# One ScalarE copy empties the value products' bank, and branch B's halves are added by accumulating loads

## The chip, the cores and the metric

The kernel runs on one core of a Trainium2 chip. The metric is device time in microseconds of one execution, as the median of several runs. Lower is better.

The engines are named as in the profile: PE is TensorE's matrix multiplication and PEld its loading of weights (the stationary operand), DVE is VectorE, ACT is ScalarE, POOL is GpSimd, and SP is SyncE, which only issues DMAs. A small q behind a name means the engine's queue of instructions (its sequencer).

## The reference, cut to what matters

One layer of a streaming encoder is computed for a prompt of 1024 frames and a sample of 64 frames. Two branches run beside each other, both fed by one input projection, and their outputs are gated, summed and projected again. Branch A is a gated linear recurrence. Branch B is causal softmax attention with 16 heads of 64 channels and a forget gate in the logits:

```python
def fox_attend(q, k, v, cq, ck, qpos, kpos):
    s = jnp.einsum('qhd,khd->hqk', q, k).astype(jnp.float32) * (HEAD_DIM ** -0.5)
    s = s + cq.astype(jnp.float32).T[:, :, None] - ck.astype(jnp.float32).T[:, None, :]
    s = jnp.where((kpos[None, :] <= qpos[:, None])[None], s, -jnp.inf)
    p = jax.nn.softmax(s, axis=-1)
    return jnp.einsum('hqk,khd->qhd', p.astype(v.dtype), v)
...
    yb = yb.reshape(B, L, W_B) * jax.nn.silu(gb)
    u = jnp.einsum('bsnw,nwd->bsnd', jnp.stack([ya, yb], axis=2), w_branch)
```

The change touches the last line of `fox_attend` (the value products) and the way from there to `yb * silu(gb)`.

## The kernel before, in words

All matrix products are made in float32 precision from operands that are split into a high and a low half: a product takes the passes high*high, high*low and low*high. High halves are written by ScalarE (a copy that rounds, line 90), low halves by a subtraction on VectorE (line 93).

**Attention.** Work is cut into 64 units `(head, q2)`: one head with 256 queries, in the order q2 = 0, 3, 1, 2 for each head. A unit has three kinds of steps on TensorE. *Scores* (lines 1212 and 1213) put logits into a PSUM bank; VectorE adds the mask and takes the least of the negated logits (line 1184), ScalarE takes the exponential (line 1191), and GpSimd inverts the row sum by a power (line 1193) and scales (line 1194). *Turns* transpose up to four blocks of 128x128 probabilities (line 1244); ScalarE writes the high half `th` of the transposed block and VectorE the low half `tl`. *Values* (`values`, lines 1265 and 1267) multiply these with the values.

In the value products the stationary operand `vv` holds the high half of the head's values in columns 0 to 63 and the low half in columns 64 to 127. So a product of 128 output rows by 256 queries holds two partial sums: rows 0 to 63 and rows 64 to 127. The output of the head is the sum of the two. Before the change, a unit's product goes into one half (256 columns) of a single PSUM bank, `pv`; `pv_half` hands the two halves out in turn. After the unit's last value step ScalarE copies rows 64 to 127 to the tile `lo`, VectorE adds rows 0 to 63 and `lo` into the tile `y` of 64 rows (line 1293), and GpSimd's queue stores `y` to DRAM, to `d_y` (line 1297). The sample's product (once for two heads, `sample_values`) is emptied by two small ScalarE copies and two small VectorE additions (line 1345).

**The planner.** ScalarE's, VectorE's and GpSimd's order in attention, and TensorE's through the whole kernel, are the order in which the program issues instructions. A loop in the program chooses the next TensorE step with estimated times. `book(engine, at, ns, do)` finds a free place of `ns` nanoseconds on an engine from time `at` on, puts the instruction on the agenda, and returns its end plus 90 ns. A step may go when its inputs are due; a unit's first value step also waits for a free room, whose times stand in `v_free` (two rooms). Where no step is due, TensorE takes a part of a *filler*: an input-projection panel (lines 179 to 181), whose results are stored and used later. The figures such as `A_LO`, `D_Y` and `G_INV` are the planner's estimates in ns and issue nothing by themselves.

**Branch A, then branch B's rows.** After attention come branch A and its eight output panels a0 to a7 (products with `ya`). Their results are multiplied by a gate on VectorE (line 1864) into four buffers `st_a`, and stored by GpSimd's queue (line 1865). Beside them the rows of branch B are prepared, eight tiles of 128 channels by 1088 frames. For each tile, `branch_in` loads `t` from `d_y` (line 1820) and `z` from `d_gb` (line 1821) on SP's queue. VectorE multiplies `t` by `z` (line 1837, or line 1855 for the first two tiles), then by sigmoid(z) (line 1826); ScalarE writes the high half `ybh` and VectorE the low half `ybl`. Tiles 0 and 1 are loaded ahead into rooms of their own; tiles 2 to 7 use two buffers (`yb_in`, `gb_in`) in turn. The first panel of branch B needs all eight tiles within its first 4 us. The weights of each panel are split into `wh` and `wl` on ScalarE and VectorE one panel ahead. In this part the scheduler of the language orders the queues of SP, VectorE, ScalarE and GpSimd by its own estimate of when each instruction is ready; only TensorE's order is that of the program. An accumulating DMA (`accum_op`) adds what it reads to what its destination holds; it is issued by GpSimd. The kernel before has eleven of them, for weights of branch A (line 297).

Of the kernel before, what the change touches and what calls it, by code (L numbers as in the profile page):

```python
# [14 lines left out]
P = 128  # L15
# [23 lines left out]
GC = 364  # L39

HOP_PE, HOP = 250.0, 90.0
D_MAX, D_LO, D_Y, D_YS = (240.0, 1.035), (130.0, 1.1), 420.0, 230.0
A_EXP, A_HI, A_LO, A_ST, A_W = (450.0, 0.85), (150.0, 0.88), 380.0, 470.0, 1060.0
G_NORM, G_INV = (260.0, 0.84), 220.0
G_DMA = 860.0
D_W = 1240.0

# [26 lines left out]
def hybrid_step(tc, a, o):  # L74
# [24 lines left out]
    d_cq = dram.tile([2, NH, DEC], F32, name="d_cq")  # L99
    d_ma = dram.tile([KT, P, T], F32, name="d_ma")  # L100
    d_mb = dram.tile([KT, P, T], F32, name="d_mb")
    d_y = dram.tile([NP, P, T], F32, name="d_y")
    d_gb = dram.tile([KT, P, T], F32, name="d_gb")
    d_ga = dram.tile([KT, P, T], F32, name="d_ga")
    d_x = [dram.tile([P, T], F32, name=f"d_x{k}") for k in range(2)]
# [930 lines left out]
    def book(engine, at, ns, do=None):  # L1036

        busy = booked[engine]
        while busy and busy[0][1] < now[0] - 20000.0:
            busy.pop(0)  # L1040
        i = 0
        while i < len(busy) and busy[i][0] < at + ns:
            at = max(at, busy[i][1])
            i += 1
        busy.insert(i, (at, at + ns))
        if do is not None:
            serial[0] += 1
            heapq.heappush(agenda, (at, serial[0], do))
        return at + ns + HOP
# [201 lines left out]
        return book("D", at, per(D_LO, n), lambda: sub(dve, tl[:, :n], tp[:, :n], f(th[:, :n])))  # L1251

    pvs = {}
    lo_free = [0.0]
    def values(u, g, h, q2):
        vv = heads_v[h]
        if g == 0:
# [27 lines left out]
            part(0, tl, start=False, stop=False)  # L1285
        high_part(0, True)
        spent(460.0)
        lo = p2.tile([HD, 256], F32, name="lo", tag="lo", bufs=1)
        y = p2.tile([HD, 256], F32, name="y", tag="y", bufs=3)

        dst = d_y[h // 2][(h % 2) * HD:(h % 2 + 1) * HD, q2 * 256:(q2 + 1) * 256]
        at = book("A", max(now[0] + HOP_PE, lo_free[0]), A_LO, lambda: copy_act(lo[:, :], pv[HD:, :256]))
        at = book("D", at, D_Y, lambda: dve.tensor_tensor(out=y[:, :], in0=pv[:HD, :256], in1=lo[:, :], op=ALU.add))
        v_free.popleft()
        v_free.append(at)
        lo_free[0] = at
        book("G", at, G_DMA, lambda: pool.dma_start(dst, y[:, :]))


# [30 lines left out]
    def sample_values(p):  # L1330
        t = smp.pop(p)
        pv = pv_half()
        for i in range(2):
            pe.matmul(pv[:, :], t["vs"][:, i, 0, :], t["pt"][:, i, :, :].rearrange("p s n -> p (s n)"),
                      start=(i == 0), stop=False)
            pe.matmul(pv[:, :P], t["vs"][:, i, 1, :], t["pt"][:, i, 0, :], start=False, stop=(i == 1))
        spent(458.0)
        ys = p2.tile([P, DEC], F32, name="ys", tag="ys", bufs=1)
        ats = []
        for j in range(2):  # L1340
            js, ks = slice(j * HD, (j + 1) * HD), slice(P + j * HD, P + (j + 1) * HD)
            ats.append(book("A", now[0] + HOP_PE, per(A_HI, HD), lambda js=js, ks=ks: copy_act(ys[js, :], pv[js, ks])))
        for j, at in enumerate(ats):
            js = slice(j * HD, (j + 1) * HD)
            at = book("D", at, D_YS, lambda js=js: dve.tensor_tensor(out=ys[js, :], in0=pv[js, js], in1=ys[js, :],
                                                                     op=ALU.add))
        book("D", at, 0.0, lambda: sp.dma_start(d_y[p][:, SEQ:], ys[:, :]))
        v_free.popleft()
        v_free.append(at)

# [19 lines left out]
    due = {}  # L1372
    s_free = deque([0.0, 0.0, 0.0])
    t_free = deque([0.0, 0.0])
    v_free = deque([0.0, 0.0])
    prs = {}
    seen = {"t": 0, "v": 0}
    last_t = {u: ("t", u, q2) for u, (h, q2) in enumerate(units)}
# [438 lines left out]
        return ybpool.tile([P, T], dt, name=name, tag=f"yb{i}{k}")  # L1817

    def branch_in(k, t, z):
        sp.dma_start(t[:, :], d_y[k])  # L1820
        sp.dma_start(z[:, :], d_gb[k])
        return t, z

# [574 lines left out]
```

## Time and profile before

| | |
|---|---|
| median of 3 runs | 1430.43 us (1429.32 to 1431.48) |
| the profiled execution | 1429.49 us, its span 1427.5 us |
| mean granted TensorE clock | 0.998 |
| busy: PE, PEld | 1410.8 us, 1358.0 us |
| busy: DVE, ACT, POOL | 899.4 us, 720.5 us, 436.5 us |
| attention's value products | from 470.9 us to 845 us |
| loads of branch B's rows (line 1820) | issued from 1017.8 us to 1090.8 us |
| first product of branch B's panels | at 1110.8 us |

The span is the time from the first to the last instruction in the profile; the execution's own time is 2.0 us more. Rows of a timeline give the start in us from the span's start, the duration in us, the engine, the line, and `out<-in`; in brackets stands idle time before the instruction, and what ended it. Rows of groups give busy time in us and mean ns of one, then idle time before. A releaser is inferred from semaphore events. Matmuls are pipelined, so the distance between two starts tells more than a matmul's own duration.

### The profile page before, as it was taken

What the parts mean: (1) busy time and instruction counts of PE and PEld (TensorE: products, weight loads), DVE (VectorE), ACT (ScalarE), POOL (GpSimd) and SP (SyncE); (2) the same over time, 40 slices, a digit from 0 to 9 for tenths busy, and PEclk for the clock granted to TensorE, in tenths of its full rate; (3) what the DMA queues carried; (4) which work ended last, traced back from release to release, by engine and by line L of the source; (5) the groups of instructions that cost most, each with busy time, mean ns of one, the idle gap of its engine ahead of it and who ended that gap; (6) DMA issues with size and microseconds to landing.
All of it is one profiled execution on the core that took longest, in us unless ns stands there. A gap on an engine that the chain in (4) does not pass through costs nothing.

```text
span 1427.5 us, 25022 instructions
## 1 busy us (share of the span) xinstructions
PE 1410.8 (99%) x9217; PEld 1358.0 (95%) x9217; DVE 899.4 (63%) x1638; ACT 720.5 (50%) x1339; POOL 436.5 (31%) x652
## 2 busy tenths in 40 slices
PE   9999999999999999999999999999999999999997
PEld 8999999999999999999999999999999999888887
DVE  5564766564432666666666656898767474777654
ACT  5423544442222666666666657777544232565443
POOL 0012322233204777768776841221011000000001
PEclk9999999999999999999999999999999999999999
DMA  6667556765247764556566545564467774224211
GB/s 225 214 133 107 150 155 193 162 180 141 85 122 194 182 130 131 137 110 151 123 150 131 84 101 106 83 101 84 165 211 264 252 237 136 113 74 150 78 48 45
DMA packets 138919, 201.20 MB, mean 141 GB/s; under 512 B 24372, under 2 KB 98844, under 8 KB 137772
## 3 DMA queue, kind: packets, MB, share of 16 engines
q1 hardware_dynamic: 119436, 158.96, 44.2%
q0 software_dynamic: 8160, 23.25, 5.9%
q10 hardware_dynamic: 11200, 17.38, 3.4%
q8 instruction: 73, 1.20, 0.3%
q14 instruction: 50, 0.41, 0.1%
HBM read 131.60 MB, written 66.36 MB: 139 GB/s over the span
## 4 chain that ended last, share of the span: by engine, by line
PE 82%; DVE 6%; DMA 5%; ACT 3%; issue 3%; POOL 1%; SPq 0%; DVEq 0%; ACTq 0%; POOLq 0%
PE quad L844 17%; PE acc L179 11%; PE acc L181 11%; PE acc L180 11%; PE q L2042 5%; PE tp L1244 4%; PE pv L1265 3%; PE s L1213 2%; PE s L1212 2%; PE pv L1267 2%; PE vacc L179 1%; PE vacc L180 1%; PE vacc L181 1%; DMA w_raw<-in_w_in 1%; PE vacc L500 1%
## 5 line engine op out<-in xcount | busy, mean ns | idle before, releaser
L179 PE MATMUL acc<-xh,wh 128*128 128x364 f32 x720 | 237.6, 330 | 0.2 <-ACT st L90 0.2
L181 PE MATMUL acc<-xh,wl 128*128 128x364 f32 x720 | 235.8, 328 | 0.0
L180 PE MATMUL acc<-xl,wh 128*128 128x364 f32 x720 | 235.8, 327 | 0.0
L179 PEld LDWEIGHTS acc<-xh,wh 128*128 128x128 f32 x720 | 135.4, 188 | 1.2 <-ACT st L90 0.5
L180 PEld LDWEIGHTS acc<-xl,wh 128*128 128x128 f32 x720 | 135.3, 188 | 0.8
L181 PEld LDWEIGHTS acc<-xh,wl 128*128 128x128 f32 x720 | 135.1, 188 | 0.0
L90 ACT ACTIVATE wh<-w_raw 128x1024 fp32r<-128x1024 f32 (+1 forms) x66 | 63.4, 962 | 86.4 <-PE quad L844 34.4
L93 DVE TENSOR_TENSOR wl<-w_raw,wh 128x1024 fp32r<-128x1024 f32 (+1 forms) x55 | 62.5, 1138 | 67.6 <-ACT wh L90 47.0
L1193 POOL TENSOR_TENSOR sm<-sm,warm 128x1 f32<-128x1 f32 x136 | 79.2, 582 | 57.0 <-ACT pb L1191 21.8
L93 DVE TENSOR_TENSOR tl<-tp,th 128x512 fp32r<-128x512 f32 x96 | 65.6, 687 | 38.7 <-ACT th L90 37.9
L844 PE MATMUL quad<-xh,wh 128*128 128x272 f32 x416 | 87.4, 291 | 1.8 <-ACT p__3330 L90 1.8
L844 PE MATMUL quad<-xl,wh 128*128 128x272 f32 x416 | 86.1, 288 | 0.0
L844 PE MATMUL quad<-xh,wl 128*128 128x272 f32 x416 | 86.0, 288 | 0.0
L1191 ACT ACTIVATE pb<-pb,nm 128x896 f32<-128x896 f32 (+1 forms) x64 | 63.3, 989 | 24.0 <-DVE nm L1184 21.3
L90 ACT ACTIVATE th<-tp 128x512 fp32r<-128x512 f32 x96 | 56.4, 592 | 31.0 <-PE tp L1244 30.3
L2338 POOL TENSOR_TENSOR junk<-ple,g_ple 128x256 f32<-128x256 f32 x4 | 3.8, 956 | 213.2 <-DVE ple L2295 213.2
L1212 PE MATMUL s<-k,q 128*128 128x128 f32 (+2 forms) x192 | 67.5, 353 | 0.0
L844 PEld LDWEIGHTS quad<-xh,wh 128*128 128x128 f32 x416 | 65.3, 188 | 2.3 <-ACT p__3330 L90 2.0
L1213 PE MATMUL s<-k,q 68*128 68x128 f32 (+2 forms) x192 | 65.3, 344 | 0.5 <-issue 0.5
L844 PEld LDWEIGHTS quad<-xh,wl 128*128 128x128 f32 x416 | 65.5, 188 | 0.0
L844 PEld LDWEIGHTS quad<-xl,wh 128*128 128x128 f32 x416 | 65.4, 188 | 0.0
L1194 POOL TENSOR_SCALAR pb<-pb,sm 128x896 f32<-128x896 f32 (+1 forms) x64 | 61.5, 962 | 6.2
(744 smaller groups left out, 4230.4 us busy)
## 6 DMA issues: line engine op xcount, KB each, us to landing
w_raw<-in_w_in SPq DMA_DIRECT2D x56, 256.0 KB
q<-d_q SPq DMA_DIRECT2D x48, 256.0 KB
k<-d_k SPq DMA_DIRECT2D x48, 256.0 KB
w_raw<-in_w_in SPq DMA_DIRECT2D x64, 128.0 KB
w_raw<-in_w_branch SPq DMA_DIRECT2D x32, 256.0 KB
wl<-w_raw POOLq DMA_DIRECT2D x11, 512.0 KB, 4.5
wraw<-in_w_in SPq DMA_DIRECT2D x20, 256.0 KB
d_k<-oh ACTq DMA_DIRECT2D x16, 272.0 KB
```

Source lines behind the costliest of these rows:

```text
L90: return act.activation(out=out, in_=in_, func=AF.Copy, scale=scale)
L93: return eng.tensor_tensor(out=out, in0=in0, in1=in1, op=ALU.subtract)
L179: pe.matmul(out, ah, bh, start=start, stop=False)
L180: pe.matmul(out, ah, bl, start=False, stop=False)
L181: pe.matmul(out, al, bh, start=False, stop=stop)
L844: pe.matmul(acc[:, c, :CW], l[:, k, :], r[:, k, c * CW:(c + 1) * CW], start=(first and k == 0 and p == 0), stop=(k == 3 and p == 2), skip_ ...
L1191: at = book("A", at, per(A_EXP, n), lambda: act.activation(out=pr[:, :n], in_=pr[:, :n], func=AF.Exp, scale=-1.0, bias=nm, accum_out=sm))
L1193: at = book("G", at, G_INV, lambda: pool.tensor_tensor(out=sm, in0=sm, in1=warm[:, :], op=ALU.pow))
L1194: return book("G", at, per(G_NORM, n), lambda: pool.tensor_scalar(out=pr[:, :n], in0=pr[:, :n], scalar1=sm, scalar2=1.0, op0=ALU.mult, op1 ...
L1212: pe.matmul(s[:, :w], t["q1"][:, q0:q0 + P], t["k1"][:, c], start=True, stop=False)
L1213: pe.matmul(s[:, :w], t["q2"][:HD + 4, q0:q0 + P], t["k2"][:HD + 4, c], start=False, stop=True)
L2042: pe.matmul(acc, l[:, k, :], r[:, k, :], start=(first and k == 0 and i == 0), stop=(k == 3 and i == 2), skip_group_check=not first)
```

## The change

The planner keeps one room for the value products, `v_free = deque([0.0])`, where it kept two; the bank and `pv_half` stay. After a unit's last value step ScalarE copies all 128 rows of the product to `y`, now a tile of 128 rows; VectorE's addition and the tile `lo` go. The store takes both halves: `d_y` has a place for each pair of heads, each head of it, 128 rows and 1024 frames. For the sample one copy of 128x256 replaces the two small ones, the two small additions read the copy in SBUF, and the result goes to a tensor of its own, `d_ys`. The planner's figure for the inversion, `G_INV`, goes from 220 to 570 ns.

In `branch_in`, the one load of `t` becomes three on SP's queue (rows 0 to 63 of the two heads' products, and the sample's columns), and two accumulating loads on GpSimd's queue add rows 64 to 127. `z` is loaded as before.

```diff
@@ -39,9 +39,9 @@
 GC = 364
 
 HOP_PE, HOP = 250.0, 90.0
-D_MAX, D_LO, D_Y, D_YS = (240.0, 1.035), (130.0, 1.1), 420.0, 230.0
-A_EXP, A_HI, A_LO, A_ST, A_W = (450.0, 0.85), (150.0, 0.88), 380.0, 470.0, 1060.0
-G_NORM, G_INV = (260.0, 0.84), 220.0
+D_MAX, D_LO, D_YS = (240.0, 1.035), (130.0, 1.1), 230.0
+A_EXP, A_HI, A_Y, A_ST, A_W = (450.0, 0.85), (150.0, 0.88), 380.0, 470.0, 1060.0
+G_NORM, G_INV = (260.0, 0.84), 570.0
 G_DMA = 860.0
 D_W = 1240.0
 
@@ -99,7 +99,8 @@
     d_cq = dram.tile([2, NH, DEC], F32, name="d_cq")
     d_ma = dram.tile([KT, P, T], F32, name="d_ma")
     d_mb = dram.tile([KT, P, T], F32, name="d_mb")
-    d_y = dram.tile([NP, P, T], F32, name="d_y")
+    d_y = dram.tile([NP, 2, P, SEQ], F32, name="d_y")
+    d_ys = dram.tile([NP, P, DEC], F32, name="d_ys")
     d_gb = dram.tile([KT, P, T], F32, name="d_gb")
     d_ga = dram.tile([KT, P, T], F32, name="d_ga")
     d_x = [dram.tile([P, T], F32, name=f"d_x{k}") for k in range(2)]
@@ -1251,7 +1252,6 @@
         return book("D", at, per(D_LO, n), lambda: sub(dve, tl[:, :n], tp[:, :n], f(th[:, :n])))
 
     pvs = {}
-    lo_free = [0.0]
     def values(u, g, h, q2):
         vv = heads_v[h]
         if g == 0:
@@ -1285,15 +1285,11 @@
             part(0, tl, start=False, stop=False)
         high_part(0, True)
         spent(460.0)
-        lo = p2.tile([HD, 256], F32, name="lo", tag="lo", bufs=1)
-        y = p2.tile([HD, 256], F32, name="y", tag="y", bufs=3)
-
-        dst = d_y[h // 2][(h % 2) * HD:(h % 2 + 1) * HD, q2 * 256:(q2 + 1) * 256]
-        at = book("A", max(now[0] + HOP_PE, lo_free[0]), A_LO, lambda: copy_act(lo[:, :], pv[HD:, :256]))
-        at = book("D", at, D_Y, lambda: dve.tensor_tensor(out=y[:, :], in0=pv[:HD, :256], in1=lo[:, :], op=ALU.add))
+        y = p2.tile([P, 256], F32, name="y", tag="y", bufs=3)
+        dst = d_y[h // 2, h % 2][:, q2 * 256:(q2 + 1) * 256]
+        at = book("A", now[0] + HOP_PE, A_Y, lambda: copy_act(y[:, :], pv[:, :256]))
         v_free.popleft()
         v_free.append(at)
-        lo_free[0] = at
         book("G", at, G_DMA, lambda: pool.dma_start(dst, y[:, :]))
 
 
@@ -1335,18 +1331,16 @@
                       start=(i == 0), stop=False)
             pe.matmul(pv[:, :P], t["vs"][:, i, 1, :], t["pt"][:, i, 0, :], start=False, stop=(i == 1))
         spent(458.0)
+        yv = p2.tile([P, 256], F32, name="y", tag="y", bufs=3)
         ys = p2.tile([P, DEC], F32, name="ys", tag="ys", bufs=1)
-        ats = []
+        at = book("A", now[0] + HOP_PE, A_Y, lambda: copy_act(yv[:, :], pv[:, :256]))
+        v_free.popleft()
+        v_free.append(at)
         for j in range(2):
             js, ks = slice(j * HD, (j + 1) * HD), slice(P + j * HD, P + (j + 1) * HD)
-            ats.append(book("A", now[0] + HOP_PE, per(A_HI, HD), lambda js=js, ks=ks: copy_act(ys[js, :], pv[js, ks])))
-        for j, at in enumerate(ats):
-            js = slice(j * HD, (j + 1) * HD)
-            at = book("D", at, D_YS, lambda js=js: dve.tensor_tensor(out=ys[js, :], in0=pv[js, js], in1=ys[js, :],
-                                                                     op=ALU.add))
-        book("D", at, 0.0, lambda: sp.dma_start(d_y[p][:, SEQ:], ys[:, :]))
-        v_free.popleft()
-        v_free.append(at)
+            at = book("D", at, D_YS, lambda js=js, ks=ks: dve.tensor_tensor(
+                out=ys[js, :], in0=yv[js, js], in1=yv[js, ks], op=ALU.add))
+        book("D", at, 0.0, lambda: sp.dma_start(d_ys[p], ys[:, :]))
 
 
 
@@ -1372,7 +1366,7 @@
     due = {}
     s_free = deque([0.0, 0.0, 0.0])
     t_free = deque([0.0, 0.0])
-    v_free = deque([0.0, 0.0])
+    v_free = deque([0.0])
     prs = {}
     seen = {"t": 0, "v": 0}
     last_t = {u: ("t", u, q2) for u, (h, q2) in enumerate(units)}
@@ -1817,7 +1811,11 @@
         return ybpool.tile([P, T], dt, name=name, tag=f"yb{i}{k}")
 
     def branch_in(k, t, z):
-        sp.dma_start(t[:, :], d_y[k])
+        for j in range(2):
+            sp.dma_start(t[j * HD:(j + 1) * HD, :SEQ], d_y[k, j][:HD, :])
+        sp.dma_start(t[:, SEQ:], d_ys[k])
+        for j in range(2):
+            pool.dma_start(t[j * HD:(j + 1) * HD, :SEQ], d_y[k, j][HD:, :], accum_op=ALU.add)
         sp.dma_start(z[:, :], d_gb[k])
         return t, z
 
```

## The prediction

> **What bounds the kernel now.** I read the page first: shares of the engines, then the chain that ended last.
>
> ```profile
> span 1427.5 us, 25022 instructions
> PE 1410.8 (99%) x9217; PEld 1358.0 (95%) x9217; DVE 899.4 (63%) x1638; ACT 720.5 (50%) x1339; POOL 436.5 (31%) x652
> PE 82%; DVE 6%; DMA 5%; ACT 3%; issue 3%; POOL 1%; SPq 0%; DVEq 0%; ACTq 0%; POOLq 0%
> ```
>
> TensorE is busy 99% of the span, 16.7 us of it idle, and carries 82% of the chain. No engine's relief shows in the end time unless TensorE waits for it. So I looked at the two stretches that the change touches, in the table by stretch: attention, and the end of branch A, where branch B's rows are loaded.
>
> ```profile
> 460.00:850.00 390.00, 388.38 (x2706) 377.93 (x2705) 247.42 (x658) 252.47 (x578) 277.72 (x455) 1.00 0.58 131
> 1060.00:1120.00 60.00, 60.00 (x362) 60.00 (x362) 38.14 (x45) 22.02 (x22) 9.18 (x17) 1.00 0.76 250
> ```
>
> Columns: stretch, length, then busy us and instructions of PE, PEld, DVE, ACT, POOL; clock, DMA share, GB/s. Attention leaves TensorE 1.6 us idle in 390, and the loading stretch none, at full clock. There, DMA is at 0.76 of its time, and POOL has 51 us free. What TensorE and its weight loads wait for in attention is the whole list below (waits, 460 to 860 us: total, times, longest), TensorE's own row first.
>
> ```profile
> PE pv L1265 <- DVE y L1293: 1.2, 4, 0.5
> PEld pv L1265 <- DVE y L1293: 2.1, 4, 0.7
> PEld pv L1267 <- DVE y L1293: 1.4, 4, 0.4
> PEld pv L1267 <- ACT lo L90: 0.2, 1, 0.2
> PEld pv L1265 <- DVE ys L1345: 0.2, 1, 0.2
> ```
>
> Every wait is for the emptying of the value products' bank. That is all this part of the change can remove: 1.2 us if only TensorE's idle counts, 3.9 us if the weight loads' does.
>
> **The emptying, part by part.** The groups by shape (460 to 850 us) price what goes and what comes.
>
> ```profile
> L90 ACT ACTIVATE lo<-pv 64x256 f32<-64x256 f32 x64 | 24.4, 382 | 20.4 <-PE pv L1265 9.4 <-PE pv L1267 7.9 <-PE pv L1336 1.2
> L90 ACT ACTIVATE ys<-pv 64x64 f32<-64x64 f32 x16 | 3.4, 213 | 0.4 <-DVE y L1293 0.3
> L90 ACT ACTIVATE pts<-tps 128x256 fp32r<-128x256 f32 x8 | 3.0, 379 | 0.1
> L1293 DVE TENSOR_TENSOR y<-pv,lo 64x256 f32<-64x256 f32 x64 | 26.4, 412 | 32.9 <-ACT lo L90 11.9 <-PE pv L1265 7.8 <-ACT st L90 3.9
> ```
>
> DVE loses its 64 additions: 26.4 us busy, and up to the 32.9 us that its queue stood still before them. Nothing on TensorE waits for another DVE operation here, so it is worth nothing by itself. ScalarE goes from 64 x 382 + 16 x 213 ns = 27.9 us to 72 copies of 128x256 at 379 ns = 27.3 us: no change. The 16 small sample additions stay on DVE and read the copy instead of PSUM; their DVE work is hidden as before.
>
> Does a single room cost anything against two? A stretch of the timeline answers.
>
> ```profile
> 504.63 0.38 ACT L90 ACTIVATE lo<-pv 64x256 f32<-64x256 f32 x1
> 505.47 0.37 PE L1265 MATMUL pv<-tl,vv 128*128 128x256 f32 x1
> 505.67 0.28 PE L1265 MATMUL pv<-th,vv 128*128 128x256 f32 x1
> 505.91 0.28 PE L1265 MATMUL pv<-th,vv 128*128 128x256 f32 x1
> 506.29 0.42 DVE L1293 TENSOR_TENSOR y<-pv,lo 64x256 f32<-64x256 f32 x1 [1.95 <-ACT st L90]
> 506.75 0.33 PE L1267 MATMUL pv<-diag0l,vv 128*128 128x128 f32 x1
> ```
>
> lo ended at 505.01, yet y began at 506.29, just after the next unit's four products of the other half; and the next product at 506.75 came right behind y's end at 506.71. The ScalarE copy that the row names as y's releaser is none that y reads; the group above names pv's products for 7.8 us of such waits. The halves already exclude each other: two rooms existed only in the planner. The Trainium skill (PSUM — Partial Sum Buffer, section "PSUM bank collisions raise a hardware error") asks for guards by bank and quadrant, not by address; the trace agrees, as y waited 1.28 us for the other half.
>
> So the new planner describes what happens. A unit's next product waits for one copy, where it could wait for copy and addition. I take the middle of 1.2 and 3.9, **-2.5 us**, since part of the weight loads' idle lies under running matmuls. New waits for a copy that ScalarE starts late lie between 0 and the 3.9 of now; I take **+0.5**, nearer the single 0.2 us wait for lo, because the copy releases the bank without an addition behind it.
>
> The planner's figures (one room, 380 and 570 ns instead of 220 for the inversion) issue nothing; they reorder the steps. POOL's power takes 554 ns (below), so 570 is nearer; TensorE now waits for no softmax, so this saves nothing. Order has a price: the first product after transposes took 0.20 us to the next (505.47 to 505.67), those after it 0.24 for two. That is 0.08 us a boundary; with the 160 value steps of the loops, a tenth of them moved gives +-1.3 us, of no sign.
>
> **Stores of the products.** Rows of 128 instead of 64 partitions, and twice the bytes. POOL's rows (instruction, its ns least, median, greatest):
>
> ```profile
> L1297 POOL DMA_DIRECT2D d_y<-y x64: 533/597/622, 474.0 to 846.1; - x64
> L1124 POOL DMA_DIRECT2D d_mb<-st x21: 556/576/638, 582.4 to 798.9; - x21
> L1193 POOL TENSOR_TENSOR sm<-sm,warm x136: 539/554/1503, 456.8 to 832.8; 128x1 f32<-128x1 f32 x136
> ```
>
> A 128-row store costs POOL 576 ns, the 64-row one 597: nothing. The extra 4 MB over 390 us is 11 GB/s on 131. y keeps three buffers, and a unit takes some 6 us (390/64), so landing is covered.
>
> **Branch B's rows.** Each of 8 row tiles had one load; it gets three on SP and two accumulating loads on POOL, which must wait for the SP loads. That is 16 more issues on SP (about 0.33 us each, 5 us over 90, in a queue that mostly waits for buffers) and 16 on POOL. Moved behind the accumulation is DVE's product L1837 (L1855 for the first two, loaded some 17 us ahead, which I take as covered). In DVE's order stand behind it the low halves of the next weights and the emptying of the a panels; on POOL the mix rows' stores queue behind a waiting accumulation.
>
> ```profile
> wl<-w_raw POOLq DMA_DIRECT2D x11, 512.0 KB, 4.5
> L297 POOL DMA_DIRECT2D wl<-w_raw x11: 853/868/917, 849.8 to 994.2; - x11
> d_mix<-st_a POOLq DMA_DIRECT2D x16, 182.0 KB, 5.7
> DMA to landing us min/median/max: 2.1/5.3/7.6
> 1068.40 0.32 SPq L1820 DMA_DIRECT2D yb_in<-d_y  x1
> 1071.50 0.47 SPq L1821 DMA_DIRECT2D gb_in<-d_gb  x1
> 1080.15 1.29 DVE L1837 TENSOR_TENSOR yb_in<-yb_in,gb_in 128x1088 f32<-128x1088 f32 x1 [4.63 <-DMA gb_in<-d_gb]
> 1083.01 1.22 DVE L93 TENSOR_TENSOR wl<-w_raw,wh 128x1024 fp32r<-128x1024 f32 x1
> 1075.11 0.34 SPq L1820 DMA_DIRECT2D yb_in<-d_y  x1
> 1084.14 1.28 DVE L1837 TENSOR_TENSOR yb_in<-yb_in,gb_in 128x1088 f32<-128x1088 f32 x1
> 1086.65 4.44 SPq L1820 DMA_DIRECT2D yb_in<-d_y  x2
> 1092.31 1.29 DVE L1837 TENSOR_TENSOR yb_in<-yb_in,gb_in 128x1088 f32<-128x1088 f32 x1
> 1101.46 1.28 DVE L1837 TENSOR_TENSOR yb_in<-yb_in,gb_in 128x1088 f32<-128x1088 f32 x1
> 1105.32 1.29 DVE L93 TENSOR_TENSOR ybl<-yb_in,ybh 128x1088 fp32r<-128x1088 f32 x1 [0.73 <-ACT ybh L90]
> 1087.11 0.33 PE L181 MATMUL acc<-yah,wl 128*128 128x364 f32 x1
> 1114.42 0.33 PE L180 MATMUL acc<-ybl,wh 128*128 128x364 f32 x1
> ```
>
> The first two rows are the accumulating loads that branch A already has, the next two POOL's mix stores in this crowded stretch (their landing, all 24, in the fourth). A pair of accumulations takes one landing and one more issue: 4.5 + 0.9 = **5.4 us** by the nearest row in kind, 2.1 + 0.5 at the low end, 7.6 + 0.9 = 8.5 at the high end. A row load alone needs at most 5.7 us where nothing crowds it (1086.65 to 1092.31) and up to 8.7 behind weights (gb_in, 1071.50 to 1080.15).
>
> At 5.7 + 5.4 = 11.1 us from issue to use, tiles 4 to 7 had 11.7, 9.0, 5.7 and 10.7 (the second of the two merged loads was issued about 1090.8). Tile 4 holds; tile 5 comes 2.1 late, tile 6 5.4. Tile 7 reuses 5's buffer: 2.1 + 0.4 = 2.5 late. Its last half, ready at 1106.6, comes at 1109.1, against TensorE's need at 1114.4: 5.3 us left. The weights wl of 1083.0 stand behind tile 4, which keeps its time. So **0** on the path. At 8.7 + 8.5 = 17.2 us, tile 4 is 5.4 late, wl ends at 1089.6 instead of 1084.2, and TensorE, needing it at 1087.1, loses 2.5. Tile 5 is 8.2 late, tile 7 8.2 + 6.5 = 14.7, so its half comes at 1121.3: 6.9 us lost in all. Below zero nothing is possible; TensorE has no idle there. Range **0 to +7**; I take 0, since the order of DVE's queue will also be laid out anew.
>
> The Trainium skill (DMA: Bandwidth & Descriptors, section "Anatomy of one DMA — SWDGE (gpsimd) path") gives 2.0 us plus bytes/436 GB/s. For 256 KB that is an estimate of 2.6 us, 3.5 with the second issue, which would leave tile 5 0.2 late. For 512 KB it would be 3.2, where the rows above show 4.5; I go by the rows.
>
> **Sum.** -2.5 + 0.5 + 0 + 0 = -2.0 us against the profiled execution, 1429.49 us (span 1427.5 and 2.0 around it): 1427.5. That execution is 0.94 under the median of the runs, 1430.43, so the forecast is **1428.4**. A measurement of this kernel tells about 0.2% from no change, 2.9 us; the forecast lies within it.
>
> **Rivals.** (a) Faster: all 3.9 us of waits go, none comes, and the order falls well (-1.3): -5.2, 1425.2. For it: every wait of attention is the one attacked. Against: TensorE's own idle there is 1.6 us.
>
> (b) Slower, the accumulation is late: load and accumulation take 17 us, +6.9 - 2.0, 1435.3. Tile 7 has 7.8 us of slack at the end, so it decides from a delay of 7.8, about 14 us from load to use with tile 5's lateness carried over. For it: DMA 0.76 busy, stores landing at up to 7.6. Against: the accumulations seen land in 4.5 to 4.7.
>
> (c) Slower, one room starves TensorE: value steps start later by the planner's 250 + 380 + 90 = 720 ns, transposes by 350, filler panels are spent early, and near the end of attention TensorE finds nothing to do. 72 emptyings, one in ten uncovered at 0.72 is +5.2; net of the -2.0, 1433.6. It decides once more than seven are uncovered. The Trainium skill (Perfetto Trace Analysis, section "Matmuls") lets independent groups rotate through banks so that emptying overlaps, which speaks for this rival; the y above shows that the halves of one bank never gave that. Against it too: some 6 us a unit, of which its value products are under 2.
>
> **Chances.** Forecast 0.55; (a) 0.22; (b) 0.13; (c) 0.10. (a) is faster, (b) and (c) slower by over 0.2%: 0.22, 0.55, 0.23. The range reaches to both sides' ends, 1425.0 to 1435.0; the forecast's own is 1427.6 to 1432.0, from +-1.3 of order and a small loss in the loads.
>
> **What would show it.** Right: no wait of TensorE for y and few, under 1 us together, for the copy; DVE about 26 us less busy; L1837 later by 2 to 5 us for some tiles with no TensorE idle between 1060 and 1120. Wrong: TensorE idle before the weights' products near 1087 or the first b panel near 1111, waits for a copy of more than 3 us, or accumulations landing in more than 8 us.

## The result and the profile after

| | before | after |
|---|---|---|
| median of 4 runs each, run together | 1429.88 us (1429.12 to 1431.48) | 1447.77 us (1446.90 to 1451.21) |
| profiled execution, its span | 1429.49 us, 1427.5 us | 1446.90 us, 1445.1 us |
| mean granted TensorE clock | 0.998 | 0.995 |

The ratio is 1.0128, 95% interval 1.0109 to 1.0147: the kernel became 18 us slower, past the upper end of the forecast's range. The page after, total and busy time of the engines:

```profile
span 1445.1 us, 25052 instructions
PE 1413.4 (98%) x9217; PEld 1362.2 (94%) x9217; DVE 876.8 (61%) x1574; ACT 712.7 (49%) x1331; POOL 451.1 (31%) x668
```

VectorE is 22.6 us less busy, as the change intends, and TensorE 31.7 us idle instead of 16.7. The table by stretch says where (columns as in the prediction):

```profile
460.00:850.00 390.00, 388.73 (x2720) 381.00 (x2719) 228.86 (x598) 245.94 (x573) 279.63 (x458) 1.00 0.62 143
1000.00:1060.00 60.00, 58.39 (x351) 58.05 (x350) 40.95 (x46) 30.25 (x31) 10.84 (x17) 1.00 0.62 180
1060.00:1120.00 60.00, 52.67 (x312) 51.37 (x310) 24.50 (x28) 16.82 (x16) 17.28 (x25) 1.00 0.93 253
1120.00:1140.00 20.00, 13.28 (x69) 12.73 (x70) 13.19 (x17) 5.07 (x6) 1.71 (x3) 0.83 0.55 159
```

Attention is no worse than before. The loading of branch B's rows, where TensorE had next to no idle time, now has 1.6 + 7.3 + 6.7 = 15.6 us of it. What TensorE waited for, first in attention (430 to 860 us, the whole list), then from 1030 to 1200 us (total, times, longest):

```profile
PE tp L1245 <- POOL pb L1195: 1.3, 1, 1.3
PE s L1214 <- DMA q<-d_rows: 0.2, 1, 0.2
```

```profile
PE acc L182 <- DVE wl L93: 9.9, 3, 7.6
PE acc L180 <- ACT ybh L90: 1.6, 1, 1.6
PE acc L180 <- ACT wh L90: 1.6, 1, 1.6
PE held L180 <- DVE st_a L1862: 1.6, 1, 1.6
PE acc L181 <- DVE ybl L93: 0.9, 1, 0.9
```

No wait for the products' bank is left. The largest wait names VectorE's low half of the weights, `wl`, which is an innocent bystander; the timeline shows what stood ahead of it. These are rows of POOL, VectorE, SP and TensorE, put in order of time; L1815 is the load of the high rows, L1818 the accumulation, L1835 the product t*z, L1863 the store of `st_a`.

```profile
1060.36 1.42 SPq L1815 DMA_DIRECT2D yb_in<-d_y  x2
1070.81 1.29 DVE L1835 TENSOR_TENSOR yb_in<-yb_in,gb_in 128x1088 f32<-128x1088 f32 x1 [7.84 <-DMA yb_in<-d_y]
1072.02 0.53 DVE L1862 TENSOR_TENSOR st_a<-acc,gate 128x360 f32<-128x360 f32 x1
1072.85 0.57 POOL L1863 DMA_DIRECT2D d_mix<-st_a  x1 [8.27 <-DVE st_a L1862]
1073.41 0.92 POOL L1818 DMA_DIRECT2D yb_in<-d_y  x1
1076.20 0.88 POOL L1818 DMA_DIRECT2D yb_in<-d_y  x1
1084.29 1.29 DVE L1835 TENSOR_TENSOR yb_in<-yb_in,gb_in 128x1088 f32<-128x1088 f32 x1 [7.32 <-issue]
1121.70 1.29 DVE L1835 TENSOR_TENSOR yb_in<-yb_in,gb_in 128x1088 f32<-128x1088 f32 x1 [9.06 <-DMA yb_in<-d_y]
1122.91 1.22 DVE L93 TENSOR_TENSOR wl<-w_raw,wh 128x1024 fp32r<-128x1024 f32 x1
1124.19 0.67 PE L182 MATMUL acc<-ybh,wl 128*128 128x364 f32 x1 [7.62 <-DVE wl L93]
```

It is a convoy. VectorE stands 7.84 us at tile 2's product, for the accumulation; `st_a` stands behind it; POOL stands 8.27 us at the store that needs this `st_a`; behind the store stand the accumulations of tile 3, whose rows SP had asked for at 1060.36; they go at 1073.41 and 1076.20, and VectorE uses tile 3 at 1084.29, 23.9 us after the load's issue. By tile 6 (1121.70) the product is so late that `wl`, queued right behind it, ends 7.6 us after TensorE wanted it. The accumulation's line, with who waited for it and its landing:

```profile
  DVE yb_in L1835: 32.8, 5
  DVE in_h L1853: 2.6, 1
DMA to landing us min/median/max: 4.9/6.9/10.0
```

VectorE waited 32.8 us in five waits, three of them marked `issue` in its rows: the trace has tile 3's second accumulation landing at 1084.21, just ahead of the product at 1084.29. About half as much, 15.6, reaches TensorE. With 1.4 us of slower products right after the longest wait (last section) these are 17.0 of the 18.5 us by which the part behind attention grew (858.72 to 1427.5, now 857.88 to 1445.1).

### The profile page after: what moved, and what is told of

It is laid out like the page before. It is cut to its first block, busy times and chain, and to the rows that moved or that the text cites. A ratio compares the mean times of both kernels' runs of the same rounds, so it can differ in the third digit from the quotient of the medians.

```text
span 1445.1 us, 25052 instructions
## 1 busy us (share of the span) xinstructions
PE 1413.4 (98%) x9217; PEld 1362.2 (94%) x9217; DVE 876.8 (61%) x1574; ACT 712.7 (49%) x1331; POOL 451.1 (31%) x668
## 4 chain that ended last, share of the span: by engine, by line
PE 75%; DMA 9%; DVE 5%; issue 5%; ACT 3%; POOL 1%; SPq 1%; ACTq 0%; DVEq 0%; POOLq 0%
PE quad L845 17%; PE acc L180 9%; PE acc L182 9%; PE acc L181 9%; PE q L2040 5%; PE tp L1245 4%; PE pv L1265 3%; PE s L1214 2%; PE s L1213 2%; PE pv L1267 2%; DMA wl<-w_raw 2%; DMA w_raw<-in_w_in 1%; PE vacc L180 1%; PE vacc L181 1%; PE vacc L182 1%
## 5 line engine op out<-in xcount | busy, mean ns | idle before, releaser
L182 PE MATMUL acc<-ybh,wl 128*128 128x364 f32 (+1 forms) x192 | 63.6, 331 | 7.6 <-DVE wl L93 7.6
```

What stands on the lines that cost most here:

```text
L182: pe.matmul(out, al, bh, start=False, stop=stop)
```

## The experiments

Medians stand beside those of the kernel before on the same chip; the ratio's 95% interval is in brackets. Theory: the accumulation, as a second transfer (a second hop) that begins when the first has landed, is the loss; rivals: its bytes, POOL's queue, the stores, the planner's order.

The loss lies behind attention, so the length of that part in the profiled execution (its span less the start of the first product `gacc`) is given as well: 568.7 us before, 587.2 after, 568.6 in e1. The part ahead of attention, which no run changes, took 451.1 to 455.3 us in the profiled executions; such differences of 2 to 4 us between two executions belong to no edit.

**Which part of the change.** e1 takes the accumulating loads out, and so leaves out the addition of the low rows; e2 puts loads of that kind alone into the kernel before, where they double the rows; e8 makes only the planner's changes.

```diff
# e1, in branch_in
-        for j in range(2):
-            pool.dma_start(t[j * HD:(j + 1) * HD, :SEQ], d_y[k, j][HD:, :], accum_op=ALU.add)
# e2, kernel before: three loads on SP and two accumulating loads of the same rows on POOL
# e8, kernel before
-G_NORM, G_INV = (260.0, 0.84), 220.0
+G_NORM, G_INV = (260.0, 0.84), 570.0
-    v_free = deque([0.0, 0.0])
+    v_free = deque([0.0])
```

> The changed kernel without its 16 accumulating loads: rows 64 to 127 of every product are stored but never added, all else is the change's. If the accumulations are the whole loss, TensorE's 15.7 us of idle between 1000 and 1220 us go and only attention's gain of about 2.6 us is left: 1427 to 1429 us against 1430 of the kernel before. If the three split loads on SP's queue or the doubled stores cost as well, it stays above 1434.

> The kernel before with only the changed way of loading branch B's rows: three loads on SP and two accumulating loads on POOL for each tile, which add the same rows once more (so those rows are doubled). Attention is untouched. If the loss belongs to these loads alone: 1447 to 1451 us, the change's time plus attention's missing gain. If the reordered attention or the larger stores had a part in it: clearly under 1445.

> The kernel before with only the planner's part: one room for the value products and 570 ns for the inversion; lo, y and VectorE's addition stay. If attention's gain of 2.6 us comes from the copy that frees the bank without an addition behind it: no gain, 1428.5 to 1432 us. If it comes from the planner's order: 1426 to 1428.

e1: 1426.32 beside 1429.31, 0.9983 [0.9972, 0.9993]. e2: 1450.24, 1.0143 [1.0127, 1.0158]. e8: 1433.81 beside 1429.75, 1.0027 [1.0018, 1.0036]. Without the accumulations the change is 3 us faster than before; with them alone the kernel is 21 us slower. So 21.5 us of loss (1447.77 to 1426.32; 18.6 behind attention in the profiled executions) belong to the accumulating loads, and the doubled stores and the split loads on SP cost nothing that shows. The planner's part alone costs 4 us, more than expected (1428.5 to 1432): the gain needs the new copy as well.

**Bytes, or the second hop?** e4 keeps the accumulations but only of 64 of the 1024 columns; e12 keeps the bytes of tiles 2 to 6, as plain loads on POOL's queue to where nobody reads them.

```diff
# e4
-            pool.dma_start(t[j * HD:(j + 1) * HD, :SEQ], d_y[k, j][HD:, :], accum_op=ALU.add)
+            pool.dma_start(t[j * HD:(j + 1) * HD, :64], d_y[k, j][HD:, :64], accum_op=ALU.add)
# e12, in branch_b; the accumulation in branch_in is out
+        if k + 1 < KT:
+            x = row_room(k + 1, "l", F32, f"x_{k}")
+            for j in range(2):
+                pool.dma_start(x[j * HD:(j + 1) * HD, :SEQ], d_y[k, j][HD:, :])
```

> The change, but every accumulating load adds only its first 64 of 1024 columns (the rest of rows 64 to 127 is left out): the same 16 DMAs, waits and queues, a sixteenth of the bytes. Landing should fall from 5 to 8 us to 2 to 3. If it is the bytes and the landing: 1428 to 1431 us. If it is mostly POOL's queue order behind the stores: still 1435 to 1442.

> No accumulation; instead, for tiles 2 to 6, POOL loads the same low rows as plain transfers into a room that nobody reads (the addition of the low rows is left out). The bytes and POOL's issues stay, the wait of one transfer for the other goes. Theory (the second hop after the load is most of the loss): 1428 to 1433. Rival (the doubled bytes and their collisions with the weights' transfers are the loss): 1442 to 1448.

e4: 1442.04 beside 1429.31, 1.0088 [1.0073, 1.0103]. e12: 1427.69 beside 1429.65, 0.9982 [0.9972, 0.9991]. With a sixteenth of the bytes, 15.7 of the 21.5 us remain (15.3 of 18.6 behind attention, 583.9 us); with the bytes of five tiles and no hop, 1.4 (568.7 us behind attention). But these loads wait for nothing, and e12 issued all ten from 1012 to 1059 us, ahead of the crowded stretch; it is e4 that tests the bytes within it. The stretch 1060 to 1120 of e12, then of e4, and the accumulations' landing in e4:

```profile
1060.00:1120.00 60.00, 60.00 (x363) 60.00 (x362) 37.30 (x43) 22.37 (x22) 8.03 (x15) 1.00 0.83 270
```

```profile
1060.00:1120.00 60.00, 53.56 (x309) 52.25 (x308) 29.10 (x30) 18.31 (x18) 15.61 (x22) 0.97 0.68 194
DMA to landing us min/median/max: 2.2/5.7/8.7
```

e4 moves less than the kernel before did (194 against 250 GB/s) and TensorE idles 6.4 us; e12, whose additional rows were issued before, moves 270 and never idles. So a loaded DMA system is not the main thing that stops TensorE here. A 16 KB accumulation lands in 5.7 us at the median, a 256 KB one in 6.9; the fall to 2 to 3 us that e4 expected did not come. (The Trainium skill, DMA: Bandwidth & Descriptors, section "Anatomy of one DMA — SWDGE (gpsimd) path", puts a fixed 2.0 us and bytes/436 GB/s, an estimate of 2.04 and 2.6 us; the 2.2 of e4's fastest agrees, the medians don't, and they decide.)

**The two buffers and the queue.** e5 gives tiles 2 to 6 rooms of their own, so that loads and accumulations go early; e3 takes the `d_mix` stores off POOL's queue; e10 does both; e11 is e5 with e4's short accumulations.

```diff
# e5
+        t = row_room(k + 1, "l", F32, f"t_{k}") if k + 1 < KT else p4.tile([P, T], F32, name="yb_in")
-        t, z = branch_in(k, p4.tile([P, T], F32, name="yb_in"), p4.tile([P, T], F32, name="gb_in"))
+        t, z = branch_in(k, t, p4.tile([P, T], F32, name="gb_in"))
# e3
-            pool.dma_start(d_mix[of][:, t0:t0 + n], s[:, :n])
+            act.dma_start(d_mix[of][:, t0:t0 + n], s[:, :n])
# e10: e5 and e3.  e11: e5 and e4
```

> The change, but tiles 2 to 6 of branch B's rows are loaded and added up in rooms of their own (the room of the next tile's low half, free until then) instead of two buffers in turn; the accumulations, their queue and their bytes stay. Theory of latency: a load and an accumulation are two hops of 5 to 9 us each in crowded DMA rings, and with two buffers the 17 to 19 us come round for every second tile; with rooms of their own the hops of several tiles overlap, so most of the loss goes: 1426 to 1433 us. Theory of POOL's queue order (an accumulation behind a store behind VectorE): the stores still stand ahead, 1438 to 1447.

> The change, but the stores of the a panels' results (line 1863) are issued by ScalarE's queue, so that POOL's queue holds the accumulations alone. Theory of the two queues (an accumulation stands in POOL's queue behind a store, the store waits for VectorE's gating, and that stands in VectorE's queue behind the product that waits for the accumulation of the tile before): most of the loss goes, 1430 to 1437 us. Rival, plain lateness (each accumulation lands 5 to 8 us after its load, with two buffers): little changes, 1444 to 1448. Rival, crowded DMA: the same 1444 to 1448.

> Branch B's tiles 2 to 6 in rooms of their own and the d_mix stores on ScalarE's queue. Theory: the two are different parts of the same loss, the wait for a buffer (about 12 us when taken away alone) and the wait in POOL's queue behind a store (about 5 us): with the loads issued early and nothing ahead of the accumulations, what is left is the doubled bytes, 1430 to 1433. Rival: with rooms of their own the accumulations are early enough, and POOL's order no longer matters: 1435 to 1437, as with the rooms alone.

> Branch B's tiles 2 to 6 in rooms of their own and only 64 of the 1024 columns accumulated (the rest of the low rows is left out). Theory: what rooms of their own leave of the loss (1435.8 against 1426.3 without accumulations) is the bytes in the stretch from 1040 to 1080, so 1428 to 1431. Rival: it is the second hop, which a short transfer has as well: 1434 to 1436.

| | us | ratio to before | behind attention, us |
|---|---|---|---|
| e5 | 1435.79 (1431.36 to 1439.13) | 1.0038 [1.0026, 1.0050] | 577.5 |
| e3 | 1442.60 | 1.0090 [1.0075, 1.0105] | 586.6 |
| e10 | 1435.03 | 1.0039 [1.0024, 1.0055] | 579.6 |
| e11 | 1426.21 | 0.9979 [0.9970, 0.9987] | 568.5 |

Started early, more than half of the loss is hidden: 12 of the 21.5 us go (9.7 behind attention). POOL's order is worth 5 us by the medians (e3), less than its theory of the two queues expected (1430 to 1437), and even that isn't shown to be POOL's: behind attention, where the edit acts, e3's profiled execution, the slowest of its four, is only 0.6 us shorter than the change's, the fastest of its four. Once the loads are early, POOL's order is worth nothing (e10; the forecast of a sum was wrong). What e5 leaves over is bytes after all: with short accumulations it is gone (e11). Moved ahead of 1060 us, the full transfers meet the first `d_mix` stores; e5's landing of those from 1040 to 1062 us, and the waits for `st_a` that follow on VectorE and TensorE:

```profile
DMA to landing us min/median/max: 9.8/10.4/10.7
DVE st_a L1863 <- DMA d_mix<-st_a: 15.5, 3, 10.6
PE held L180 <- DVE st_a L1863: 2.4, 1, 2.4
```

In e11 the same landing is 3.1 to 7.9 us. So here the hop and the bytes were each hidden, but not by one move: early enough for the hop was into the stores.

**The sum without a second hop.** All of these keep the whole computation. e6 has own rooms, plain loads of both parts on SP, and the addition on VectorE. e14 keeps the two buffers, loads the low rows by POOL into the room of the tile's later high half, and adds on VectorE (tiles 0 and 1 still accumulate); e15 adds on POOL; e16 does the first two tiles that way as well; e17 lets e16's low rows take turns in two rooms.

```diff
# e14, tiles 2 to 7
-            pool.dma_start(t[j * HD:(j + 1) * HD, :SEQ], d_y[k, j][HD:, :], accum_op=ALU.add)
+            pool.dma_start(x[js, :SEQ], d_y[k, j][HD:, :])
+        x = row_room(k, "h", F32, f"x_{k}")
+            dve.tensor_tensor(out=t[:, :SEQ], in0=t[:, :SEQ], in1=x[:, :SEQ], op=ALU.add)
# e15: pool.tensor_tensor.  e16: x for tiles 0 and 1 too.  e17: x = row_room(7, "hl"[k % 2], ...)
```

> As the run before, but rows 64 to 127 come by two plain loads on SP's queue into a second room and VectorE adds them (8 additions of 128x1024, about 1.2 us each, 10 us of VectorE): one hop instead of two, the same bytes from DRAM. Theory of latency: 1426 to 1430 us, the gain of attention of about 2.6 us kept. If the doubled bytes alone crowd the rings so that weights come late: above 1433.

> As the change, but for branch B's tiles 2 to 7 POOL loads the low rows as plain transfers into a second room (the one of the tile's own later high part), not waiting for the load of the high rows, and VectorE adds the two ahead of t*z; the first two tiles keep their accumulating loads. Theory (neither the bytes nor the addition is the loss, only that one transfer waits for the other): the time of the run with the bytes alone, 1427.7, plus at most 2 for six additions of some 1.1 us on VectorE, which is busy 37 of 60 us there: 1426 to 1430 us, so both kernels would be equalled or beaten. Rival 1: the rival by bytes, which own rooms with separate adding showed (1437.4): 1435 to 1440. Rival 2: the six additions in VectorE's queue ahead of the weights' low parts make TensorE wait as the accumulation did: 1432 to 1438.

> The same with the six additions on POOL. Theory: the chain of a tile gets a second engine and POOL's slower addition (an estimate of 2 us each), but VectorE's queue still waits for it in order: 1427 to 1433. Rival: POOL's queue, which also issues the d_mix stores and the next low rows, is blocked by an addition that waits for its loads, so the loads come late again: 1434 to 1442.

> As the run with two plain loads and VectorE's additions, with the first two tiles done the same way, so that no accumulating transfer into SBUF is left in branch B; the whole computation is kept. Theory: the 3.7 us that TensorE still waited at 1047.8 (for st_a, behind the first two tiles' accumulations of 7 to 10 us landing) go, and what is left over the run without accumulations is below 2 us: 1426 to 1430. Rival: that wait comes from the additional bytes and additions between 1020 and 1050, not from the second hop: it stays, 1431 to 1435.

> As the run with two plain loads for all tiles, but the low rows of tiles 2 to 7 take turns in two rooms (those that hold the first two gates until about 1050), so that their loads are spread as the two buffers' are and no longer issued together from 1036 to 1049; the whole computation is kept. Theory (what is left, 1.9 us of idle TensorE at 1047, is the d_mix stores landing 8 us late behind those loads): the wait goes, 1426 to 1429 us, faster than before. Rival: POOL's queue, standing at a load that waits for its room, holds up the d_mix stores behind it, so that st_a runs out of buffers: 1431 to 1437.

| | us | ratio to before | behind attention, us |
|---|---|---|---|
| e6 | 1437.37 | 1.0053 [1.0041, 1.0065] | 581.8 |
| e14 | 1433.43 (1431.29 to 1435.26) | 1.0026 [1.0014, 1.0038] | 575.0 |
| e15 | 1433.37 (1429.64 to 1437.04) | 1.0025 [1.0016, 1.0035] | 577.1 |
| e16 | 1430.57 (1426.84 to 1435.89) | 1.0003 [0.9990, 1.0016] | 572.4 |
| e17 | 1439.25 | 1.0061 [1.0047, 1.0074] | 586.7 |

e16 computes what the change computes, with the same bytes and stores, in 17 us less. Its low rows have no second hop, and as their rooms are free they also start early, from 1011 to 1058 us; how much each of the two is worth isn't separated. TensorE's first row of waits from 860 to 1200 us in e14, then in e16:

```profile
PE held L180 <- DVE st_a L1869: 3.7, 1, 3.7
```

```profile
PE held L180 <- DVE st_a L1867: 1.9, 1, 1.9
```

The expectation of e14 (1426 to 1430) was too low by this wait, which stands behind the accumulations of the first two tiles; e16, without them, has half of it. e15's additions on POOL (2.7 us each) did no better than e14's on VectorE. What is left in e16 stands where its low rows are loaded in a bunch, from 1036 to 1049 us, with `d_mix` stores landing at a median of 8.2 us from 1040 to 1062 (6.6 in e12). A halved clock follows this wait and makes it dearer by some 1.6 us (last section). e17 was to cure that and brought the convoy back, by its rival: POOL stood 16.0 us at low rows that waited for a room (four waits for VectorE), and the `d_mix` stores behind it. It has no second hop, and yet its profiled execution, the slowest of its six, is behind attention as long as the change's (586.7 and 587.2 us): rows that come late and take turns in two rooms are enough. e6 missed its forecast (1426 to 1430), but it is no test of early loads: the scheduler spread them, tile 4's at 1070.4 us where e5 has it at 1043.9. TensorE waited 3.0 us for `st_a` and 3.8 for `ybh` there; why e6 is 8 us slower than before stays open.

**Adding elsewhere.** e7 adds the halves in DRAM by an accumulating store behind the first; e13 adds them there by eight accumulating transfers, meant for the recurrence's stage; e9 adds in SBUF on VectorE after the copy and stores one row, as before.

```diff
# e7
+        at = book("G", at, G_DMA, lambda: pool.dma_start(dst, y[:HD, :]))
+        book("G", at + 5000.0, G_DMA, lambda: pool.dma_start(dst, y[HD:, :], accum_op=ALU.add))
# e13, one for each tile, in the loop of the recurrence
+        pool.dma_start(d_y[k][:, :HD, :], d_y[k][:, HD:, :], accum_op=ALU.add, max_dma_last_dim=4096)
# e9, in values
+        at = book("D", at, 420.0, lambda: dve.tensor_tensor(out=ya[:, :], in0=y[:HD, :], in1=y[HD:, :], op=ALU.add))
```

> Attention as changed, but the halves are added at the store: rows 0 to 63 go to the layout of the kernel before by a plain store, and rows 64 to 127 are added to it in DRAM by an accumulating store that POOL issues at a planned 5 us later; y has four buffers; branch B's rows come by one load as in the kernel before. If branch B's loads are the whole loss, this keeps attention's gain: 1425.5 to 1429 us. If POOL's queue cannot bear 64 more issues of 0.6 us and their waits in attention (it is at 72%), TensorE waits for probabilities: above 1432.

> The bank's copy and the stores stay as in the change; the low rows are added to the high ones in DRAM, by one accumulating transfer for each tile that POOL issues in the recurrence's stage (about 870 to 1010 us, DMA share 0.5 there), and branch B loads the sum with two loads and d_ys, and no second hop. Theory (the addition costs only where it stands between a load and its reader): attention keeps its gain, branch B's loading is that of the run without accumulations, 1426 to 1428 us. Rival 1: accumulating transfers disturb the weights' transfers wherever they run, 8 of 5 to 10 us each, so that TensorE waits for weights between 870 and 1010: 1429 to 1434. Rival 2: the stores' layout or the loads in halves cost something that the run without accumulations hid: 1429 to 1431.

> The bank is still one room emptied by one ScalarE copy, but the halves are added by VectorE between two SBUF tiles after the bank is free, and one row is stored and loaded as before the change; nothing is accumulated. Theory (the copy that frees the bank gives the gain, the accumulating loads take it back): attention ends about 2.6 us earlier and branch B's loading is as before, so 1426 to 1428 us, with VectorE back near 899 us busy. Rival 1: the gain in attention came from VectorE's 22.6 us less work, not from the bank: then it is lost again, 1429 to 1430. Rival 2: one room in the planner costs what the run with one room alone showed (+4): 1431 to 1434.

e7: 1465.04 beside 1429.75, 1.0240 [1.0222, 1.0258]; attention itself became longer, its last value product at 879 us instead of 845. POOL stood 27.4 us, in ten waits, at accumulating stores for a first store to land: a second hop again, in the queue that attention needs. e13: 1547.40 beside 1429.99, 1.0821 [1.0806, 1.0836]. The scheduler put its transfers at 518.6 to 949.9 us, most of them in attention, so it didn't test the quieter stage. It tells two things: such a transfer of 512 KB from DRAM to DRAM is slow, and the stores of `y` behind it land late, so that ScalarE waited 47.5 us for room in `y`. Its landing, and TensorE's longest waits from 460 to 1000 us:

```profile
DMA to landing us min/median/max: 25.7/28.6/31.8
PE pv L1265 <- ACT y L90: 37.0, 4, 12.0
PE s L1213 <- DVE nm L1185: 24.4, 2, 13.1
```

e9: 1431.52 (1428.98 to 1434.22) beside 1429.65, 1.0008 [0.9998, 1.0017]: no gain. The two theories of attention's gain part here: the bank is freed by the copy, and no wait for it is left, but VectorE has its addition back. (e9 also has two buffers of `y` where the change has three, and its time lies in the range of its second rival, the price of one room; neither is ruled out.) TensorE's waits in e9 from 430 to 860 us, all of them:

```profile
PE s L1212 <- DVE nm L1184: 2.1, 1, 2.1
PE s L1213 <- DMA q<-d_rows: 1.7, 1, 1.7
PE s L1213 <- issue: 0.7, 1, 0.7
```

## Why the prediction was wrong, point by point

**The emptying** (-2.5 + 0.5): right in size. First product of the scores and first of the branch after attention (`gacc`), before and then after:

```profile
452.20 0.22 PE L1212 MATMUL s<-k,q 128*128 128x128 f32 x1
858.72 0.33 PE L179 MATMUL gacc<-uh,g_h 128*128 128x364 f32 x1
```

```profile
453.93 0.22 PE L1213 MATMUL s<-k,q 128*128 128x128 f32 x1
857.88 0.33 PE L180 MATMUL gacc<-uh,g_h 128*128 128x364 f32 x1
```

406.52 us became 403.95: -2.57. The twelve other runs that keep this attention took 403.5 to 405.4 us for the stretch, and e2, with the attention of before, 406.5. The copy took what was forecast (72 x 378 ns = 27.2 us), and no wait for it appears. The reason given is only half shown. The prediction held VectorE's relief to be worth nothing by itself; e9, without bank waits and with the addition, took 407.02 us for the stretch. So the waits for the bank may be gone and others come, unless VectorE is relieved too. How the 2.6 us divide between bank, VectorE and the order of steps stays open.

**One room and the new figures** (no cost but +-1.3): rival (c) did not come about, yet e8 shows that such a price exists: with one room, the new figure of the inversion and the old emptying the stretch takes 862.08 - 452.13 = 409.95 us, 3.4 more than before. Which of the two figures costs it isn't separated.

**Stores** (0): right. The store's median on POOL is 591 ns against the forecast 576, and e1 with all of them is faster than before.

**Branch B's rows** (0, range 0 to +7): the step that failed; it measured 18.5 us in the profiled executions and some 21 by the medians. The landing of an accumulation was not far off: 4.5 us forecast and 7.6 at the high end, 6.9 at the median and 10.0 at most measured, with 0.9 for the issue as forecast. Two things built on it were.

First, the sum of load and accumulation. At 11.1 to 17.2 us from issue to use the forecast reached 0 to +7; the trace has 20.4 for tile 2 (1050.39 to 1070.81) and 23.9 for tile 3 (1060.36 to 1084.29). Between the two transfers lay a third item that the sum did not hold. Tile 3's accumulations were issued 13.1 and 15.8 us after its first load, where the forecast gave the load 8.7 at most; the rest, 4 to 7 us, they stood in POOL's queue behind `d_mix` stores. The prediction named that queue the other way round only, the stores behind a waiting accumulation. Both happen, and with VectorE's queue they close a ring: accumulation, t*z, `st_a`, store, next accumulation. But this is the smaller part. In e3 no store stands in POOL's queue, and tile 3 still takes 18.9 us:

```profile
1061.52 1.16 SPq L1815 DMA_DIRECT2D yb_in<-d_y  x2
1080.44 1.29 DVE L1835 TENSOR_TENSOR yb_in<-yb_in,gb_in 128x1088 f32<-128x1088 f32 x1 [8.16 <-DMA yb_in<-d_y]
```

Second, and larger, the lateness was not handed on. The forecast took tiles 4 to 7 with the loads' times of the kernel before, and let only tile 7 inherit lateness, from tile 5 through the buffer. But each load from tile 4 on waits for the low half `ybl` of the tile two before, whose buffer it takes. SP's row of these waits in the kernel before, and there the loads and products of tiles 2 and 3, which the forecast left out:

```profile
SPq L1820 <- DVE ybl L93: 8.3, 4, 3.7
1049.30 1.17 SPq L1820 DMA_DIRECT2D yb_in<-d_y  x1
1062.21 1.28 DVE L1837 TENSOR_TENSOR yb_in<-yb_in,gb_in 128x1088 f32<-128x1088 f32 x1
1059.89 0.44 SPq L1820 DMA_DIRECT2D yb_in<-d_y  x1
1069.42 1.28 DVE L1837 TENSOR_TENSOR yb_in<-yb_in,gb_in 128x1088 f32<-128x1088 f32 x1
```

At the forecast's own 17.2 us tile 2 is already 4.3 late and tile 3 7.7; tiles 4 and 6 inherit the one, 5 and 7 the other, and the last half comes 22.4 us late. That is an estimate of 14.6 us lost, from these rows and the prediction's, instead of 6.9. Measured, the products of tiles 2 to 7 come 8.6, 14.9, 17.1, 22.5, 29.4 and 24.2 us later than before. The experiments put the two in the same order: e3, which cuts the ring at POOL, saves 5 us by the medians and 0.6 behind attention in the profiled executions; e5, which takes the buffers out of it, 12 and 9.7.

Its further assumption, "0, since the order of DVE's queue will also be laid out anew", failed too: the scheduler left `wl` behind t*z, and TensorE paid 7.6 us for that at one place. Rival (b) had the mechanism, an accumulation that comes late; its turning point, about 14 us from load to use, was passed by five of the six tiles (13.9 to 23.9 us). Its price, +6.9, held one late tile and not the convoy. The first two tiles, "covered" by 17 us, made VectorE wait 2.6 us, and TensorE 1.6 for `st_a` behind it.

**The signs.** Of those for "wrong", two came: TensorE idle for weights and at the first b panel (9.9 us in three waits for `wl`, 7.6 of them before that panel's third product), and landings above 8 us. Long waits for the copy did not. That VectorE would be about 26 us less busy was nearly so (22.6).

## What to carry to other kernels

An addition moved from an engine into a DMA is not free because the DMA system has room: it is a second round trip that starts when the first has landed, here 5.7 us at the median for 16 KB and 6.9 for 256 KB, and it puts a wait into the in-order queue of the engine that issues it and of the engine that reads it. Before pricing it, walk the queues in a ring: what stands behind the reader, what does that release, and does the next transfer's issue stand behind that? If it closes through buffers that are taken in turn, start at the first tile and add the lateness up along those that share a buffer. Plain loads into rooms of their own and an addition at the reader (e16) cost 17 us less here for the same bytes. No version that computes everything beat the kernel before by more than can be measured.

## What the runs showed of the hardware beyond that

After the idle 7.62 us TensorE's clock was halved for a while: the granted clock is 0.50 from 1120.4 to 1127.0 us. Rows of the kernel after, behind the row of 1124.19 above:

```profile
1124.66 0.51 PE L180 MATMUL acc<-ybh,wh 128*128 128x364 f32 x1
1124.96 0.51 PE L181 MATMUL acc<-ybl,wh 128*128 128x364 f32 x1
...
1127.27 0.33 PE L180 MATMUL acc<-ybh,wh 128*128 128x364 f32 x1
1127.44 0.33 PE L181 MATMUL acc<-ybl,wh 128*128 128x364 f32 x1
```

Products start every 0.30 us instead of 0.17 for some 2.9 us, which adds 1.4 us to the wait. The Trainium skill (TensorE: Matmul & The Clock Gate, section "Part 1: The HAM clock gate") says the clock falls to half after an idle window of about 3.4 us and recovers after as much work; this stretch roughly agrees, with 7.6 us idle and 2.9 us of slow products. Other runs don't, and they decide: in e16 an idle of 1.95 us (to 1046.15) was enough, and in e9 2.14 us (to 808.28) were not. The stretches behind the two, e16's first (the clock is the third number from the end):

```profile
1046.50:1049.80 3.30, 3.30 (x13) 3.30 (x12) 0.92 (x3) 0.00 (x0) 2.60 (x5) 0.50 0.89 203
808.00:810.00 2.00, 1.72 (x8) 1.45 (x9) 1.67 (x8) 1.68 (x6) 1.49 (x3) 1.00 0.39 103
```

So a wait of 2 us may cost nearly twice its length: e16's products start every 0.30 us up to 1049.7, which adds some 1.6 us. What decides between the two, these runs don't show.

VectorE's addition of two SBUF operands in e9 is dearer than the one of PSUM and SBUF before (the group of e9 in attention):

```profile
L1293 DVE TENSOR_TENSOR ya<-y 64x256 f32<-64x256 f32 x64 | 32.2, 504 | 16.8 <-ACT y L90 10.5 <-DMA d_y<-ya 4.4
```

504 ns in the mean against 412. Nine of the 64 took 0.69 to 1.30 us, and each of these ran beside a GpSimd instruction of the softmax or of the values' low halves for 0.4 us or more; none before took over 0.42. The Trainium skill (SBUF — State Buffer, section "Terms") has VectorE and GpSimd share a pair of SBUF ports, one shutting the other out; these nine agree with it, though others of the 64 overlapped such instructions and weren't slower.
